# Every SBUF tile that the matmuls read at 32 modulo 256 bytes, in a one-core encoder block

## The chip, the core and the metric

The kernel runs on one core of a Trainium2 chip. The metric is device time in microseconds (us) of one execution; a kernel is run several times and the median is taken. Beside these runs there is one profiled execution, whose trace gives the start and end of each instruction.

## The reference, cut to what matters

One layer over 512 tokens of 1024 features:

```python
x = x + 0.5 * swiglu_ffn(rms_norm(x, ffn1_norm), ffn1_w13, ffn1_w2)      # D_FF = 2816
h = rms_norm(x, mix_norm)
a, g, q, k, v, fl = split(h @ w_in)        # 512 | 512 | 512 | 512 | 512 | 8
y_conv = silu(layer_norm(depthwise_conv31(a * sigmoid(g)) + conv_b))
y_attn = softmax(q k^T / 8 + cum[t] - cum[s], causal) @ v      # 8 heads of 64
#   cum = cumsum(log_sigmoid(fl + forget_b))
y = concat(rms_norm(y_conv, out_norm_conv), rms_norm(y_attn, out_norm_attn))
x = x + y @ w_out
x = x + 0.5 * swiglu_ffn(rms_norm(x, ffn2_norm), ffn2_w13, ffn2_w2)
out = rms_norm(x, final_norm)
```

## The kernel before, in words

**Data.** Features lie on the 128 partitions, tokens along the row. A 512-token row of fp32 is 2048 bytes of a partition. The stream x is eight such tiles. Every matmul operand is kept as two fp32r tiles, a rounded high part and the rest (`xh`/`xl` for the input, `whi`/`wlo` for weights), and a product is the sum of three matmuls for each block of 128 rows: high by high, low by high, high by low. In `product` the weight block (128x128, 512 bytes of a partition) is the operand that is loaded into TensorE (weight load, PEld), and the input row is the one that streams (512 columns, or 256 in `seven`). In `values` it is the other way round: blocks of `xh`/`xl` are loaded and 260 columns of weights stream.

**Weights.** A "unit" is one 512 KB block of weights. SP's queue brings it into one of three `raw` buffers, ScalarE (ACT) casts it into one of two `whi` buffers, VectorE (DVE) subtracts to one of two `wlo` buffers; units take the buffers in turn. The units of `values` hold four blocks of 260 columns, so their rows are 4160 bytes long where all others have 4096.

**Stages**, by the trace's time: both FFNs (about 17 to 365 us and 590 to 950 us) alternate gate and up products (`f1g`, `f1u`, `f2g`, `f2u`: 24 matmuls of 512 columns each) with `seven`, which forms the down projection of eight hidden tiles from seven half-size products (`f1p`, `f2p`: 84 matmuls of 256 columns); the last six hidden tiles go down in plain products (`f1o`, `f2o`). Between them stands the mixer: four `conv_tile`s (`pg`, `pa`), `values` (`pv`), four `attention`s of two heads (`pq`, `pk`, scores `s`, transposes `pt`, output `po`), `conv_norm`, and the output projection (`wo`). Two of the convolutions run on DVE (`conv`), two as ACT taps that POOL adds up (`tap`, `acc`), beside all of `values` and attention.

**Order.** Every operation is recorded first; `Plan.schedule` then emits all engines' streams by priced costs and buffer availability, and each engine runs its stream in order. Matmul products follow each other in the recorded order (`in_turn`).

**Addresses.** The allocator lays tiles out one behind another in the order of their first use: a tag's buffers lie side by side, each as long as the tag's longest tile. The three `raw` buffers start at 36640, which is 32 modulo 256. After them the 4160-byte buffers and the conv inputs `u0` to `u3` (542 columns, 2176 bytes with padding) shift all that follows. In the built program this gives, modulo 256:

| tile | before | changed |
|---|---|---|
| `whi`, two buffers | 224, 32 | 32, 32 |
| `wlo`, two buffers | 96, 160 | 32, 32 |
| `xh0` to `xh7`, `xl1` to `xl7` | 224 | 32 |
| `xl0` | 96 | 32 |
| `vt` (a unit held whole: `w2` in `f1g1`, A22 of `seven`) | 224, both halves | 32, both halves |
| hidden tiles and sums of `seven`, `yh`/`yl`, `q`, `k` | 224, some 96 | 32 |

All blocks inside a tile lie at multiples of 512 bytes from its start, except in `values`, where blocks of 260 columns are 1040 bytes apart. The constants `ones` and `sel` lie at 128 and stay there.

The functions that the change touches, and what calls them:

Of the kernel before, what the change touches and what calls it, by code (L numbers as in the profile page):

```python
# [36 lines left out]
P = 128  # L37
T = 512
D = 1024
KD = D // P  # L40
# [6 lines left out]
DC = 512  # L47
NC = DC // P
TAPS = 31
H = 8  # L50
HD = 64
NT = T // P
VC = 260
# [26 lines left out]
G_CW = 52  # L80
G_FB = G_CW + NC * TAPS
N_G = G_FB + H

# [275 lines left out]
def block_kernel(ctx: ExitStack, tc, x_d, w13a, w2a, wag, wvf, wqk, wo, w13b, w2b, par_d, out_d):  # L359
# [9 lines left out]
    def tile_(shape, tag, name, bufs=1, dt=F32):  # L369
        return plan.tile(sb, shape, dt, tag, name, bufs)  # L370
# [4 lines left out]
    def product_bank(name):  # L375
        return bank("mm", name, 3)
# [40 lines left out]
    def down(w2, js, d):  # L417
        pieces = []
        for j in js:
            half, k = divmod(j, HALF)  # L420
            if pieces and pieces[-1][1] == KD * half + d and pieces[-1][3] == k:
                pieces[-1][3] = k + 1
            else:
                pieces.append([w2, KD * half + d, k, k + 1])
        return pieces

    units = []
    for w13, w2 in ((w13a, w2a), (w13b, w2b)):
        for g in range(len(GROUPS) + 1):
            for i, j in enumerate(GROUPS[g] if g < len(GROUPS) else [None] * (KD // 2)):  # L430
                if j is not None:
                    units += [([(w13, 2 * j + n, 0, KD)], P) for n in range(2)]
                if g and i < KD // 2:
                    units += [(down(w2, GROUPS[g - 1], d), P) for d in (2 * i, 2 * i + 1)]
        if w13 is w13a:
            for piece in ORDER.split():
                n = int(piece[1:] or 0)
                units += {"c": [([(wag, 2 * n + i, 0, KD)], P) for i in range(2)],
                          "v": [([(wvf, i, 0, KD // 2)], VC) for i in range(4)],
                          "a": [([(wqk, 2 * n + i, 0, KD)], P) for i in range(2)],  # L440
                          "n": [], "w": [([(wo, 2 * n + i, 0, KD)], P) for i in range(2)]}[piece[0]]
    taken = [0]
# [115 lines left out]
    def product(ps, w, ah, al):  # L558

        hi, lo = w  # L560
        n = len(ah)
        first = None
        for k in range(n):
            step = plan.join("PE", first)
            if first is None:
                first = step
                if taken[0] > 3 or ready == []:
                    in_turn(step)
            PE.matmul(ps, hi[:, k], ah[k], start=k == 0, stop=False)
            PE.matmul(ps, hi[:, k], al[k], start=False, stop=False)  # L570
            PE.matmul(ps, lo[:, k], ah[k], start=False, stop=k == n - 1)
            plan.join(None)
        stream[:] = [step]
# [208 lines left out]
    def conv_tile(i):  # L782
        pg, pa = product_bank(f"pg{i}"), product_bank(f"pa{i}")
        product(pg, unit(), xh, xl)
        if not mix:
            mix["rstd"] = st.rstd()
        rstd = mix["rstd"]
        gn, an = tile_([P, T], "ew", f"gn{i}", BUFS["ew"]), tile_([P, T], "ew", f"an{i}", BUFS["ew"])
        V.tensor_mul(gn, pg, rstd)
        S.activation(gn, gn, AF.Sigmoid)  # L790
        product(pa, unit(), xh, xl)
        V.tensor_mul(an, pa, rstd)
        u = tile_([P, TAPS - 1 + T], f"u{i}", f"u{i}")
        G.memset(u[:, :TAPS - 1], 0.0)
        V.tensor_mul(u[:, TAPS - 1:], an, gn)
        acc = slot(16 + i, f"acc{i}")
        a = bank("cv", f"conv{i}") if i in DVE_CONV else acc
        for j in range(TAPS):
            w = par[:, G_CW + i * TAPS + j:G_CW + i * TAPS + j + 1]
            bias = par[:, G_CB + i:G_CB + i + 1]  # L800
            if i in DVE_CONV and j == 0:
                V.tensor_scalar(a, u[:, 0:T], w, bias, ALU.mult, ALU.add)
            elif i in DVE_CONV:
                V.scalar_tensor_tensor(a, u[:, j:j + T], w, a, ALU.mult, ALU.add)
            elif j == 0:
                S.activation(a, u[:, 0:T], AF.Identity, scale=w, bias=bias)
            else:
                t = tile_([P, T], "tap", f"tap{i}_{j}", 2)
                S.activation(t, u[:, j:j + T], AF.Copy, scale=w)
                G.tensor_add(a, a, t)  # L810
        if a is not acc:
            S.copy(acc, a)
        plan.urgency = 0.0
        conv[i] = acc


    vt = tile_([P, NT, H * HD], "vt", "vt")
    zf = tile_([P, NT, H], "zf", "zf")
    cum = []

    def values():
        plan.urgency = URGENT_V
        pr = bank("misc", "pr", MISC)
        PE.transpose(pr[:, :P], st.compact, ident)
        rcol = tile_([P, NT], "rcol", "rcol")
        V.tensor_copy(rcol, pr[:, 0:P:32])
        plan.urgency = 0.0
        for c in range(2):
            pv = [product_bank(f"pv{c}_{t}") if t < 2 else bank("s", f"pv{c}_{t}", 2) for t in range(NT)]
            for kh in range(2):  # L830
                hi, lo = unit()
                for t in range(NT):
                    ts_ = slice(t * P, (t + 1) * P)
                    o = pv[t][:, :VC]
                    head = None
                    for k in range(KD // 2):
                        kk = kh * (KD // 2) + k
                        step = plan.join("PE", head)
                        if head is None:
                            head = step  # L840
                            in_turn(step)
                        PE.matmul(o, xh[kk][:, ts_], hi[:, k], start=kk == 0, stop=False)
                        PE.matmul(o, xh[kk][:, ts_], lo[:, k], start=False, stop=False)
                        PE.matmul(o, xl[kk][:, ts_], hi[:, k], start=False, stop=kk == KD - 1)
                        plan.join(None)
                    stream[:] = [step]
            plan.urgency = URGENT_V
            for t in range(NT):
                rc = rcol[:, t:t + 1]
                S.activation(vt[:, t, 4 * HD * c:4 * HD * (c + 1)], pv[t][:, :4 * HD], AF.Copy, scale=rc)  # L850
                V.scalar_tensor_tensor(zf[:, t, 4 * c:4 * c + 4], pv[t][:, 4 * HD:VC], rc,
                                       par[:, G_FB + 4 * c:G_FB + 4 * c + 4], ALU.mult, ALU.add)
            plan.urgency = 0.0

        plan.urgency = URGENT_LF
        lf, e1, e2, e3 = (tile_([P, NT, H], n, n) for n in ("lf", "e1", "e2", "e3"))
        ps = plan.tile(pp, [P, 16, NT, H], F32, "pt", "e", PT)
        p1, p2, p3, p4 = (ps[:, n] for n in range(4))  # L860
        V.scalar_tensor_tensor(e1, zf, -1.0, zf, ALU.mult, ALU.min)
        S.activation(p1, e1, AF.Exp)
        plan.join("V")
        V.tensor_scalar(p2, p1, 2.0, None, ALU.add)
        V.reciprocal(e2, p2)
        V.tensor_mul(p3, p1, e2)
        V.tensor_mul(e1, p1, e2)
        V.tensor_mul(p4, p3, e1)
        V.tensor_scalar(e3, p4, 1.0 / 17.0, None, ALU.mult)
        for n in (15, 13, 11, 9, 7, 5, 3):  # L870
            V.scalar_tensor_tensor(e3, e3, 1.0 / n, p4, ALU.add, ALU.mult)
        V.scalar_tensor_tensor(e3, e3, 1.0, p3, ALU.add, ALU.mult)
        V.tensor_scalar(p2, zf, 0.0, None, ALU.min)
        V.scalar_tensor_tensor(lf, e3, -2.0, p2, ALU.mult, ALU.add)
        plan.join(None)


        for g in range(2):
            lfs = tile_([P, NT, P], "ew", f"lfs{g}", BUFS["ew"])
            G.memset(lfs, 0.0)  # L880
            V.tensor_copy(lfs[:, :, 0::32], lf[:, :, 4 * g:4 * g + 4])
            pc = bank("misc", f"pc{g}", MISC)
            plan.join("PE")
            for t in range(NT):
                PE.transpose(pc[:, t * P:(t + 1) * P], lfs[:, t], ident)
            plan.join(None)
            cs = slot((21, 14)[g], f"cum{g}")
            V.tensor_tensor_scan(cs, one, pc, 0.0, ALU.mult, ALU.add)

            rows = plan.tile(dr, [4, T], F32, f"cum{g}", f"cumd{g}")  # L890
            with plan.urgent(500.0):
                Q.dma_start(out=rows, in_=cs[0::32, :])
            cum.append(rows)

        plan.urgency = 0.0
# [211 lines left out]
```

## Time and profile before

| | |
|---|---|
| median of 3 runs | 967.07 us (966.13 to 968.39) |
| profiled execution | 966.01 us |
| its span in the trace | 964.3 us (1.7 us lie around it) |
| TensorE busy | 945.4 us, 98% of the span |
| DVE, ACT, POOL busy | 664.4, 420.7, 152.5 us |
| DMA | 91.19 MB, mean 95 GB/s |

Matmuls overlap in their pipeline, so a matmul's duration in the trace is longer than the time that it takes of TensorE. What it takes is the distance from its start to the start of the next one. In this text that distance is called a step.

### The profile page before, as it was taken

To read this page: it belongs to the slowest core of one execution; us is meant where nothing else is said; L and a number is where in the kernel's file an instruction comes from. 1 tells how busy PE (TensorE), PEld (TensorE's weight loads), DVE (VectorE), ACT (ScalarE), POOL (GpSimd) and SP (SyncE) were. 2 spreads that over 40 slices of the span, in tenths; PEclk is the share of its full clock that TensorE was granted. 3 is DMA by queue.
4 is the path that set the end of the run, shared out by engine and by line. 5 is a ranking of instruction groups with operands and counts; after the bars stand their busy time and mean duration, and the time that the engine had idled before them with its cause. 6 is when DMAs were issued, how large, how long until landed. Compare 5 with 4: busy or idle time off the path is not lost.

```text
span 964.3 us, 13408 instructions
## 1 busy us (share of the span) xinstructions
PE 945.4 (98%) x5233; PEld 790.3 (82%) x5233; DVE 664.4 (69%) x1050; ACT 420.7 (44%) x656; POOL 152.5 (16%) x134
## 2 busy tenths in 40 slices
PE   9999999999999999998999999999999999999995
PEld 7888888888998888896666777888898888999884
DVE  6655887657777465889988866555777756766454
ACT  7433433334333246666769645333443333333232
POOL 1000211001121001997732000000111001111000
PEclk9999999999999999999999999999999999999998
DMA  7223332223322232222211112223332222332122
GB/s 253 79 87 103 116 108 91 88 88 103 127 99 83 66 111 92 88 89 86 90 67 53 57 67 88 88 93 104 114 106 93 83 89 87 132 110 104 50 66 88
DMA packets 31455, 91.19 MB, mean 95 GB/s; under 512 B 3352, under 2 KB 10648, under 8 KB 31392
## 3 DMA queue, kind: packets, MB, share of 16 engines
q1 hardware_dynamic: 31392, 90.33, 27.6%
q8 instruction: 41, 0.67, 0.3%
q14 instruction: 22, 0.18, 0.1%
HBM read 88.21 MB, written 2.11 MB: 94 GB/s over the span
## 4 chain that ended last, share of the span: by engine, by line
PE 89%; DVE 4%; POOL 3%; ACT 2%; issue 1%; DMA 0%; SPq 0%; DVEq 0%; POOLq 0%; ACTq 0%
PE f2g L235 13%; PE f2u L235 13%; PE f1u L235 13%; PE f1g L235 13%; PE f2p L235 8%; PE f1p L235 8%; PE wo L235 5%; PE f1o L235 3%; PE f2o L235 3%; POOL acc L235 3%; PE pk L235 2%; PE pg L235 1%; PE pq L235 1%; PE pa L235 1%; PE po L235 1%
## 5 line engine op out<-in xcount | busy, mean ns | idle before, releaser
L235 ACT CAST whi<-raw 128x1024 fp32r<-128x1024 f32 (+3 forms) x153 | 151.6, 991 | 311.4 <-issue 135.8
L235 DVE TENSOR_TENSOR wlo<-raw,whi 128x1024 fp32r<-128x1024 f32 (+3 forms) x153 | 185.9, 1216 | 21.5 <-ACT whi L235 18.3
L235 POOL TENSOR_TENSOR acc<-acc,tap 128x512 f32<-128x512 f32 x60 | 89.0, 1485 | 86.8 <-ACT tap L235 83.2
L235 PE MATMUL f1u<-xl,whi 128*128 128x512 f32 x176 | 69.4, 394 | 0.4 <-DVE xl L235 0.3
L235 PE MATMUL f2u<-xh,wlo 128*128 128x512 f32 x176 | 69.7, 396 | 0.0
L235 PE MATMUL f1u<-xh,wlo 128*128 128x512 f32 x176 | 69.6, 396 | 0.0
L235 PE MATMUL f2g<-xh,wlo 128*128 128x512 f32 x176 | 69.6, 396 | 0.0
L235 PE MATMUL f2g<-xl,whi 128*128 128x512 f32 x176 | 69.6, 395 | 0.0
L235 PE MATMUL f1u<-xh,whi 128*128 128x512 f32 x176 | 69.4, 394 | 0.0
L235 PE MATMUL f2g<-xh,whi 128*128 128x512 f32 x176 | 69.2, 393 | 0.0
L235 PE MATMUL f2u<-xh,whi 128*128 128x512 f32 x176 | 69.2, 393 | 0.0
L235 PE MATMUL f2u<-xl,whi 128*128 128x512 f32 x176 | 69.1, 393 | 0.0
L235 PE MATMUL f1g<-xl,whi 128*128 128x512 f32 x168 | 66.6, 396 | 0.0
L235 PE MATMUL f1g<-xh,wlo 128*128 128x512 f32 x168 | 66.5, 396 | 0.0
L235 PE MATMUL f1g<-xh,whi 128*128 128x512 f32 x168 | 66.3, 394 | 0.0
L235 DVE TENSOR_TENSOR f2un<-f2u,rstd_f2in 128x512 f32<-128x512 f32 x22 | 15.2, 691 | 65.8 <-PE f2u L235 65.8
L235 POOL TENSOR_TENSOR f2S<-raw 128x512 f32<-128x512 f32 x8 | 10.4, 1298 | 311.9 <-DMA raw<-w2b 296.9
L235 DVE TENSOR_TENSOR f1un<-f1u,rstd_in 128x512 f32<-128x512 f32 x22 | 15.2, 690 | 55.6 <-PE f1u L235 55.6
L235 ACT ACTIVATE tap<-u,par 128x512 f32<-128x512 f32 x60 | 42.5, 720 | 22.2 <-POOL acc L235 22.1
L235 POOL TENSOR_TENSOR f1S<-raw 128x512 f32<-128x512 f32 x8 | 10.4, 1299 | 263.3 <-DMA raw<-w2a 227.0
L235 DVE SCALAR_TENSOR_TENSOR conv<-u,par,conv 128x512 f32<-128x512 f32 x60 | 44.9, 749 | 0.8
L235 PEld LDWEIGHTS f1u<-xl,whi 128*128 128x128 f32 x176 | 33.0, 188 | 8.9 <-DVE xl L235 1.2
(406 smaller groups left out, 2408.0 us busy)
## 6 DMA issues: line engine op xcount, KB each, us to landing
raw<-w13b SPq DMA_DIRECT2D x44, 512.0 KB, 3.4
raw<-w13a SPq DMA_DIRECT2D x42, 512.0 KB, 3.5
raw<-w2a SPq DMA_DIRECT2D x16, 512.0 KB, 3.5
raw<-w2b SPq DMA_DIRECT2D x16, 512.0 KB, 3.4
raw<-wag SPq DMA_DIRECT2D x8, 512.0 KB, 3.5
raw<-wqk SPq DMA_DIRECT2D x8, 512.0 KB, 3.4
raw<-wo SPq DMA_DIRECT2D x8, 512.0 KB, 3.5
raw<-w2a SPq DMA_DIRECT2D x16, 192.0 KB, 2.4
```

Of the source, the lines that this page charges most:

```text
L235: ins = getattr(target, method)(*real, **kw)
```

## The change

The loads of `values` are cut into eight units of two blocks (`[128, 2, 260]`, 2080 bytes of a partition) in place of four units of four, so that the longest tile in `raw`, `whi` and `wlo` is 4096 bytes; and the conv inputs are allocated with 576 columns (2304 bytes), of which 542 are used as before. Every tile from `raw` on then starts at 32 modulo 256. The arithmetic and the number of matmuls stay as they were; `values` has four more loads, casts and subtractions of half the size.

```diff
+U = 576
...
-                          "v": [([(wvf, i, 0, KD // 2)], VC) for i in range(4)],
+                          "v": [([(wvf, i, k, k + 2)], VC) for i in range(4) for k in (0, 2)],
...
-        u = tile_([P, TAPS - 1 + T], f"u{i}", f"u{i}")
+        u = tile_([P, U], f"u{i}", f"u{i}")[:, :TAPS - 1 + T]
...
-            for kh in range(2):
+            for kh in range(4):
                 hi, lo = unit()
                 for t in range(NT):
...
-                    for k in range(KD // 2):
-                        kk = kh * (KD // 2) + k
+                    for k in range(2):
+                        kk = kh * 2 + k
```

The planner then orders the mixer anew; up to the first matmul of `values` all five streams are as before, but for names. Two places are shown. On ACT, at the start of `values`, before (`whi` is a unit's cast, `tap` a product of a convolution, `gn` a sigmoid):

```order
L235 CAST whi_3586<-raw_3466 128x1040
L235 ACTIVATE gn_3589<-gn_3589 128x512
L235 ACTIVATE tap_18_3601<-u_2775,par 128x512
L235 ACTIVATE tap_19_3606<-u_2775,par 128x512
L235 ACTIVATE tap_20_3620<-u_2775,par 128x512
L235 ACTIVATE tap_21_3631<-u_2775,par 128x512
L235 CAST whi_3640<-raw_3514 128x1040
L235 ACTIVATE tap_22_3657<-u_2775,par 128x512
L235 ACTIVATE tap_23_3685<-u_2775,par 128x512
L235 ACTIVATE tap_24_3704<-u_2775,par 128x512
L235 CAST whi_3713<-raw_3563 128x1040
```

In the changed kernel the same stretch of ACT's stream, up to the fourth half unit:

```order
L236 CAST whi_3586<-raw_3466 128x520
L236 ACTIVATE tap_18_3591<-u_2775,par 128x512
L236 ACTIVATE gn_3589<-gn_3589 128x512
L236 ACTIVATE tap_19_3606<-u_2775,par 128x512
L236 ACTIVATE tap_20_3617<-u_2775,par 128x512
L236 ACTIVATE tap_21_3630<-u_2775,par 128x512
L236 CAST whi_3637<-raw_3514 128x520
L236 ACTIVATE tap_22_3651<-u_2775,par 128x512
L236 CAST whi_3682<-raw_3563 128x520
L236 ACTIVATE tap_23_3687<-u_2775,par 128x512
L236 ACTIVATE tap_24_3712<-u_2775,par 128x512
L236 CAST whi_3720<-raw_3603 128x520
```

The second cast of `values` stands behind tap 21 in both, but there it brings half a unit, and it is needed after half as many matmuls.

On TensorE, behind `values`, where the transposes `pc` of the forget gates (`lfs`) stand among the matmuls of the first key product `pk`, before:

```order
L235 MATMUL pk_4010<-xh_125,whi_3949 128x512
L235 MATMUL pk_4010<-xl_132,whi_3949 128x512
L235 MATMUL pk_4010<-xh_125,wlo_3963 128x512
L235 MATMUL pc_4026<-ident,lfs_3651 128x128 x4
L235 MATMUL pk_4010<-xh_137,whi_3949 128x512
```

In the changed kernel at the same place of TensorE's stream:

```order
L236 MATMUL pk_4035<-xh_125,whi_3980 128x512
L236 MATMUL pk_4035<-xl_132,whi_3980 128x512
L236 MATMUL pk_4035<-xh_125,wlo_3994 128x512
L236 MATMUL pk_4035<-xh_137,whi_3980 128x512
L236 MATMUL pk_4035<-xl_143,whi_3980 128x512
L236 MATMUL pk_4035<-xh_137,wlo_3994 128x512
L236 MATMUL pc_4058<-ident,lfs_3648 128x128 x4
```

The transposes moved behind three more matmuls of `pk`.

## The prediction

> **What bounds the kernel now.** First the page: busy time of the engines, the granted clock in 40 slices, and the chain of work that ended last.
>
> ```profile
> span 964.3 us, 13408 instructions
> ...
> PE 945.4 (98%) x5233; PEld 790.3 (82%) x5233; DVE 664.4 (69%) x1050; ACT 420.7 (44%) x656; POOL 152.5 (16%) x134
> ...
> PEclk9999999999999999999999999999999999999998
> ...
> PE 89%; DVE 4%; POOL 3%; ACT 2%; issue 1%; DMA 0%; SPq 0%; DVEq 0%; POOLq 0%; ACTq 0%
> ```
>
> TensorE is busy nearly throughout at a full clock and makes up 89% of the chain. Then the same by stage (columns: window, its length, busy time and count of each engine, clock, DMA share, GB/s):
>
> ```profile
> 17.60:365.00 347.40, 347.40 (x1841) 297.43 (x1840) 233.78 (x341) 130.72 (x187) 24.45 (x25) 1.00 0.29 98
> 412.00:450.00 38.00, 33.73 (x232) 30.98 (x231) 34.62 (x63) 25.66 (x39) 34.89 (x26) 0.96 0.24 84
> 450.00:590.00 140.00, 137.58 (x893) 99.09 (x892) 116.73 (x243) 93.76 (x183) 42.34 (x36) 1.00 0.21 72
> 590.00:940.00 350.00, 350.00 (x1858) 299.42 (x1851) 224.96 (x327) 123.62 (x176) 21.40 (x16) 1.00 0.28 94
> ```
>
> In both FFNs TensorE never stops, DVE is busy 67% and 64%, DMA below 30%. So there only the step of a matmul counts, and the feeding engines have room for a faster one. In the mixer TensorE stops for 4.3 us in one window (38.00 less 33.73) and for 2.4 us in the next. The chain, in order of time, gives the length of whole products:
>
> ```profile
> 53.00 5.56 PE f1g L235 x24
> 58.56 5.55 PE f1u L235 x24
> ...
> 108.53 10.01 PE f1p L235 x84
> ...
> 129.65 9.91 PE f1p L235 x84
> ...
> 332.57 33.32 PE f1o L235 x144
> ```
>
> A step of 512 columns is 5.555/24 or 33.32/144, both 231.4 ns; one of 256 columns is 9.96/84, 118.6 ns. The program issues 2364 of the first kind in the FFNs (four times 22 products of 24, 144 in `f1o`, 108 in `f2o`), 576 in the mixer (16 products of 24, 192 in `wo`), and 1344 of the second kind (16 times 84).
>
> **Whether the place of an operand matters.** One product in the trace has all its weights at the residue of its input: `f1g1`, whose unit is held in `vt`, both halves at 224, as are `xh` and `xl`. Beside it an ordinary gate product, weights at 224 and 96; starts of first matmuls and of the matmul after the last (columns: start, duration, instruction):
>
> ```profile
> 18.14 0.39 PE L235 MATMUL f1g<-xh,w 128*128 128x512 f32 x1
> ...
> 21.13 0.39 PE L235 MATMUL f1g<-xl,w 128*128 128x512 f32 x1
> ...
> 23.40 0.39 PE L235 MATMUL f1g<-xh,w 128*128 128x512 f32 x1
> 23.62 0.40 PE L235 MATMUL f1u<-xh,whi 128*128 128x512 f32 x1
> ...
> 75.05 0.40 PE L235 MATMUL f1g<-xh,whi 128*128 128x512 f32 x1
> ...
> 80.61 0.39 PE L235 MATMUL f1u<-xh,whi 128*128 128x512 f32 x1
> ```
>
> The uniform product takes 23.62 less 18.14, 5.48 us or 228.3 ns a step, and its last ten steps (21.13 to 23.40) 227 ns. The mixed one takes 5.56 us. Nothing else differs: same shapes, same input, same clock. The products with weights at 32 and 160 (`f1u` above, 5.55) are no faster than those at 224 and 96, so at 512 columns the residue of the weights alone changes nothing; that all are equal does. At 256 columns it is otherwise. Twelve matmuls each: weights at 224 and 96, all at 224 (A22, from `vt`), weights at 32 and 160:
>
> ```profile
> 109.80 0.28 PE L235 MATMUL f1p<-f10h,whi 128*128 128x256 f32 x1
> ...
> 111.22 0.28 PE L235 MATMUL f1p<-f10h,f1S 128*128 128x256 f32 x1
> ...
> 115.53 0.28 PE L235 MATMUL f1p<-f10h,f1A 128*128 128x256 f32 x1
> ...
> 116.96 0.27 PE L235 MATMUL f1p<-f10h,f1S 128*128 128x256 f32 x1
> ...
> 130.90 0.28 PE L235 MATMUL f1p<-f10h,whi 128*128 128x256 f32 x1
> ...
> 132.26 0.28 PE L235 MATMUL f1p<-f10h,f1S 128*128 128x256 f32 x1
> ```
>
> These are 1.42, 1.43 and 1.36 us: 118.3, 119.2 and 113.3 ns a step. Uniform at 224 gains nothing here; weights at 32 and 160 do, by 5.0 ns.
>
> **The change part by part.** No row has the streaming operand anywhere but at 224 or 96 in `product`, so a uniform 32 is an extrapolation.
>
> *512 columns, FFNs.* Ends: 227 ns (settled) and 228.3 (with the first, slower half of `f1g1`, whose first input row `xl0` lies at 96). I take 227.5, the middle, since `xl0` now lies with the rest, while each new product may have to settle: 2364 x (231.4 - 227.5) = 9.2 us less, all on the path.
>
> *512 columns, mixer.* 576 x 3.9 is 2.2 us; TensorE waits there for others at many places, so I count half, 1.1 us less (ends 0 and 2.2).
>
> *256 columns.* The nearest row is the uniform one, 119.2 against the mean 118.6: 1344 x 0.6 = 0.8 us more. The other end is 113.3: 1344 x 5.3 = 7.1 us less.
>
> *Values.* Four units become eight. A cast or subtraction of 520 columns lies between these rows:
>
> ```profile
> L235 ACT CAST whi<-raw 128x1040 fp32r<-128x1040 f32 x4 | 4.2, 1048 | 0.0
> ...
> L235 DVE TENSOR_TENSOR wlo<-raw,whi 128x1040 fp32r<-128x1040 f32 x4 | 4.9, 1237 | 0.0
> ...
> raw<-w2a SPq DMA_DIRECT2D x16, 192.0 KB, 2.4
> ...
> raw<-wvf SPq DMA_DIRECT2D x4, 520.0 KB, 3.4
> ```
>
> With the half at no less than half of these, and a few tenths of fixed cost each, ACT and DVE get some 0.7 us more each (an estimate), in the window where DVE is busy 34.62 of 38 us. The four more loads land in 2.4 to 3.4 us each, no longer than the 2.9 us that TensorE takes for a half unit, and three `raw` buffers run ahead; SP's queue issues them where it issued the large ones, ahead of the same `wqk` loads. What is not hidden is the buffer: there are two `whi`, and the second half unit can be cast only when `pa` has left its buffer, as the first half starts on TensorE, and when ACT has passed tap 21:
>
> ```profile
> 411.98 0.28 PE L235 MATMUL pv<-whi,xh 128*128 128x260 f32 x1
> ...
> 435.49 0.39 PE L235 MATMUL pq<-xh,whi 128*128 128x512 f32 x1
> ...
> 414.96 1.04 ACT L235 CAST whi<-raw 128x1040 fp32r<-128x1040 f32 x1
> ...
> 416.04 1.24 DVE L235 TENSOR_TENSOR wlo<-raw,whi 128x1040 fp32r<-128x1040 f32 x1
> ```
>
> `values` takes 23.51 us for 192 matmuls, 2.94 us a half unit. The first half is done at 414.9; the second's low part is ready when the DVE row of 416.04, halved, is done: about 416.7. TensorE waits 1.8 us, and perhaps 1 us more at the third, whose subtraction stands behind the long `u` product on DVE. So `pq` starts some 2 to 3 us late. Behind it stands the longest wait of the kernel:
>
> ```profile
> 437.71 0.46 ACT L235 ACTIVATE vt<-pv,rcol 128x256 f32<-128x256 f32 x1
> 438.06 1.04 ACT L235 CAST whi<-raw 128x1024 fp32r<-128x1024 f32 x1
> 439.12 1.28 ACT L235 ACT_TABLE_LOAD   x1
> ...
> 446.70 0.43 DVE L235 COPY lfs<-lf 128x16 f32<-128x16 f32 x2
> ...
> 447.10 1.11 PE L235 MATMUL pc<-ident,lfs 128*128 128x128 f32 x4 [4.02 <-DVE lfs L235]
> ```
>
> TensorE stands 4.02 us for the forget gates, whose chain starts with the last `vt` on ACT, 437.71, itself two us behind the last `pv`. Work that reaches this place 2 to 3 us late finds the wait shorter, not the end later. Three more `pk` matmuls now go ahead of `pc` (0.7 us). Ends: 0.7 us less, and 3 us more if the gates' chain is late by as much; I take 0. If the cover goes, the next in line are the rows behind `pc` (`pk`, then the scores of the first head), at the price just given.
>
> *Order of the mixer behind `pc`.* The planner reorders attention and conv_norm. The window 450 to 590 has 2.4 us of idle TensorE: I take 0 with 2.4 us to either side.
>
> *Conv inputs.* Longer tiles, same instructions: nothing.
>
> The sum is -9.2 - 1.1 + 0.8 = -9.5 us on the profiled execution's 966.01, 956.5. The median of the runs is 1.06 us above that execution, so I forecast 957.5.
>
> **A rule that speaks against it.** The Trainium skill, TensorE: Matmul & The Clock Gate, section Back-to-back issue gap, gives a single stream's gap as N/2.4 + 2.5 ns, with no term for where an operand lies; by it the change would save nothing (the second rival below), and a step of 512 columns would be 215.8 ns. The trace does not agree: the steps above are 228 to 231 ns and differ with the place alone.
>
> **Rivals.**
> *The place 32 is itself better.* The 5.0 ns that weights at 32 and 160 gained at 256 columns may come on top at all widths: 5.0 x (2364 + 1344) = 18.5 us, so about 939. For it: the flat 113.3. Against: at 512 columns these weights gained nothing.
> *Nothing happens.* `f1g1` may be fast for another reason: its two halves lie in one tile 4096 bytes apart, and it runs right behind the start-up. Then only the small terms are left: 966 to 967.5. Against: the slow steps of ordinary products occur also late, with an undisturbed stream.
> *Slower: streaming rows at 32 cost.* The streaming operand was never at 32. If starting there costs each matmul what weights at 224 cost against 32, 5.0 ns with no gain from uniformity, it is 5.0 x 3708 = 18.5 us more, about 985.5; from 0.5 ns on, 1.9 us, it makes the kernel measurably slower. For it: no row excludes it. Against: in `values` the streaming weights pass through all residues in steps of 16 bytes and the mean step there, 122 ns for 260 columns, is no longer than that of `f1p` in proportion.
> *Values and the gate chain* are too small to decide: 3 us more, with the main gain, is 960.5.
>
> **How the numbers follow.** The uniform gain as summed: 0.55 (950 to 961). The better place on top: 0.13 (932 to 948). Nothing: 0.18 (964 to 968). Slower: 0.14 (969 to 985). A range from 938 to 967.5 leaves out the lower half of the second case and the last. This kernel's no-change band is 0.2%, 1.9 us. Faster by more: 0.55 + 0.13 + a quarter of the third, 0.72; within: 0.13; slower: 0.15.
>
> **What would show it.** After: `f1g`, `f1u` products of 5.44 to 5.48 us in the chain, in both weight buffers alike; `f1p` at 9.9 to 10.1; `pq` starting later against the end of `pa`, the wait before `pc` shrunk to about 1 to 2 us. The prediction is wrong if the gate and up products stay at 5.55, or if `f1p` and `f1g` shorten both by 5 ns a step.

## The result

The changed kernel takes 960.93 us (median of 6 runs, 958.22 to 961.76) against 967.21 us for the kernel before on the same chip (6 runs, 966.13 to 968.39): a ratio of 0.9932, interval 0.9917 to 0.9946. The forecast was 957.5 us. The profiled execution of after took 961.41 us. From its page, the span, the busy time of the engines and the chain of work that ended last:

```profile
span 959.7 us, 13428 instructions
...
PE 937.7 (98%) x5233; PEld 791.0 (82%) x5233; DVE 671.6 (70%) x1054; ACT 422.1 (44%) x660; POOL 151.5 (16%) x134
...
PE 85%; DVE 9%; ACT 2%; issue 2%; DMA 1%; SPq 0%; DVEq 0%; ACTq 0%
```

TensorE is busy 7.7 us less (945.4 before) for the same 5233 matmuls, but the span is shorter by 4.6 us only. DVE is busy 7.2 us more, and its share of the chain went from 4% to 9%: the end now depends on DVE at places where it did not. The chain of after in order of time (start, length, what):

```profile
32.17 5.44 PE f1g L236 x24
37.61 5.44 PE f1u L236 x24
...
108.33 10.07 PE f1p L236 x84
118.41 5.47 PE f1g L236 x24
...
129.31 10.07 PE f1p L236 x84
...
330.57 32.64 PE f1o L236 x144
363.21 2.04 PE pg L236 x9
...
589.54 0.68 PE f2g L236 x3
...
944.51 0.85 PE rb_out L236 x8
```

Gate and up products are 5.44 us in both weight buffers, where one gave 5.56 and the other 5.55. A step of 512 columns is 32.64/144 or 5.44/24, both 226.67 ns (231.4 before). The 84 matmuls of `seven` take 10.07 us in either buffer (10.01 and 9.91 before): the 113.3 ns steps of the second buffer are gone and nearly all are 120 ns. The rows of the chain of before that mark the same places:

```profile
30.79 5.56 PE f1g L235 x24
...
365.90 2.09 PE pg L235 x9
...
589.14 0.68 PE f2g L235 x3
...
948.36 0.85 PE rb_out L235 x8
```

And around `values` and the transposes of the gates, the timeline of TensorE in after (in brackets the idle time ahead, and what ended it):

```profile
408.46 0.28 PE L236 MATMUL pv<-whi,xh 128*128 128x260 f32 x1
...
413.89 0.39 PE L236 MATMUL pv<-wlo,xh 128*128 128x260 f32 x1 [1.97 <-DVE wlo L236]
...
435.25 0.39 PE L236 MATMUL pq<-xh,whi 128*128 128x512 f32 x1
...
446.44 0.71 PE L236 MATMUL pc<-ident,lfs 128*128 128x128 f32 x4 [2.86 <-DVE lfs L236]
```

From the starts in these rows, and those of `pv` and `pc` before (411.98 and 447.10), the span divides so, in us:

| stretch | before | after | difference |
|---|---|---|---|
| to the second gate product | 30.79 | 32.17 | +1.4 |
| from there to the end of `f1o` | 335.11 | 331.04 | -4.1 |
| convolutions, to the first `pv` | 46.08 | 45.25 | -0.8 |
| `pv` to `pc` | 35.12 | 37.98 | +2.9 |
| `pc` to the first `f2g` | 142.04 | 143.10 | +1.1 |
| FFN2, to `rb_out` | 359.22 | 354.97 | -4.2 |
| to the end | 15.94 | 15.19 | -0.8 |

The two FFNs gave 8.3 us, where 8.4 was forecast (two errors that nearly cancel, see below). The mixer, where a gain of 1.1 was forecast, lost 3.1. The start-up belongs to the execution more than to the kernel: over the profiles of this study the second gate product begins anywhere from 30.7 to 33.0 us.

### The profile page after: what moved, and what is told of

Its sections match the earlier page's. It is cut to its first block, busy times and chain, and to the rows that moved or that the text cites. A ratio compares the mean times of both kernels' runs of the same rounds, so it can differ in the third digit from the quotient of the medians.

```text
span 959.7 us, 13428 instructions
## 1 busy us (share of the span) xinstructions
PE 937.7 (98%) x5233; PEld 791.0 (82%) x5233; DVE 671.6 (70%) x1054; ACT 422.1 (44%) x660; POOL 151.5 (16%) x134
## 4 chain that ended last, share of the span: by engine, by line
PE 85%; DVE 9%; ACT 2%; issue 2%; DMA 1%; SPq 0%; DVEq 0%; ACTq 0%
PE f2g L236 13%; PE f2u L236 12%; PE f1u L236 12%; PE f1g L236 12%; PE f2p L236 8%; PE f1p L236 8%; PE wo L236 4%; PE f1o L236 3%; PE f2o L236 3%; DVE conv L236 3%; DVE wlo L236 2%; PE pk L236 1%; PE s L236 1%; PE pg L236 1%; PE pa L236 1%
## 5 line engine op out<-in xcount | busy, mean ns | idle before, releaser
L236 DVE TENSOR_TENSOR wlo<-raw,whi 128x1024 fp32r<-128x1024 f32 (+3 forms) x157 | 190.0, 1210 | 19.4 <-ACT whi L236 17.5
L236 PEld LDWEIGHTS f1u<-xh,whi 128*128 128x128 f32 x176 | 33.0, 188 | 8.4 <-ACT xh L236 1.5
```

What stands on the lines that cost most here:

```text
L236: ins = getattr(target, method)(*real, **kw)
```

## Whether the place is the cause, and which place

Every kernel below is compared with the kernel before in the same batch (967.1 to 967.3 us there). First the change in two halves. The places alone, with whole units in `values`; the rows of the three weight tags are made 4352 bytes long (17 times 256), so that they keep the residue (the address modulo 256; `block_tile` allocates `[P, ROW]` and uses the first 4 x 260 columns):

```diff
+ROW = 1088
...
-    "v": [([(wvf, i, k, k + 2)], VC) for i in range(4) for k in (0, 2)],
+    "v": [([(wvf, i, 0, KD // 2)], VC) for i in range(4)],
...
-        hi = tile_(shape, "whi", f"whi{n}", SPLITS, F32R)
+        hi = block_tile(shape, "whi", f"whi{n}", SPLITS, F32R)
```

> All operands at 32 modulo 256 as in the changed kernel, but values keeps its four units of four blocks (its raw, whi and wlo tiles are lengthened to 4352 bytes, 17 times 256, of which 4160 are used). Theory A (the equal residue gives the gain of the FFNs, and the halved units of values cost the mixer some 3 to 5 us): gate and up products stay at 5.44 us, the 2.2 us wait at the second unit of values is gone, 956 to 958 us. Rival B (the mixer's loss comes from its rows being reordered at all, not from the halved units): 960 to 962 us, the waits only at other places.

It took 958.47 us (4 runs, 958.43 to 959.06), ratio 0.9911 (0.9897 to 0.9924), 2.5 us less than the changed kernel. Its chain, and the waits of TensorE in the mixer (from 365 to 592 us; us in total, times, longest):

```profile
107.42 10.07 PE f1p L242 x84
117.50 5.47 PE f1g L242 x24
...
329.66 32.64 PE f1o L242 x144
```

```profile
PE pc L242 <- DVE lfs L242: 4.0, 1, 4.0
...
PE pv L242 <- DVE wlo L242: 0.6, 2, 0.4
```

The FFN products are those of after to the hundredth, and the wait of `values` is nearly gone. The time is half a microsecond above what theory A gave and 1.5 us below the range of rival B. The halves alone, at the old addresses (`ROW` of 1040 gives tiles of 4160 bytes as before):

```diff
-U = 576
+ROW = 1040
+U = 542
```

> Addresses as before the change (tiles of raw, whi and wlo 4160 bytes long, conv inputs of 542 columns), but values in eight units of two blocks. Theory A: the FFN products stay at 5.55 us and the mixer loses the 3 to 5 us of waits, without the gain of its own matmuls: 970 to 973 us. Rival B (the halved units cost nothing; the loss in the mixer comes from faster matmuls that wait for others): 966 to 968 us.

969.01 us (11 runs, 967.02 to 970.74), ratio 1.0020 (1.0010 to 1.0029). The chain has the old products, the waits of TensorE in the mixer are new:

```profile
31.53 5.56 PE f1g L242 x24
...
109.28 10.01 PE f1p L242 x84
130.40 9.91 PE f1p L242 x84
```

```profile
PE pc L242 <- DVE lfs L242: 2.8, 1, 2.8
PE pt L242 <- DVE sm L242: 2.7, 1, 2.7
PE pv L242 <- DVE wlo L242: 1.9, 2, 1.7
```

So the two parts of the change work against each other: the places bring 8.7 us, and halving the units of `values` costs 1.8 us by itself and 2.5 us on top of the places. That cost is smaller than was expected (969.01 lies between the ranges of the two theories), but the new waits and the sign are those of theory A.

Next, whether 32 is special. Two kernels are the changed one with a constant tile, `mean`, made 224 and 64 bytes longer, which puts the blocks and rows of all products at 0 and at 96 (the second has 32 + 16 where the diff has 32 + 56):

```diff
-    mean = tile_([P, 32], "mean", "mean")
+    mean = tile_([P, 32 + 56], "mean", "mean")[:, :32]
```

> The changed kernel with everything from raw on 224 bytes further, so that all operands lie at 0 modulo 256. Theory A (only equality counts): steps of 226.7 ns at 512 columns and 120.0 at 256 as in the changed kernel, 959 to 963 us. Rival C (the place itself counts, and a row that starts on a boundary has no first part that is short): 220 ns at 512 and 113.3 at 256, the same 6.7 ns less at both, which is 25 us in the FFNs: 933 to 940 us.

> The changed kernel with everything from raw on 64 bytes further: all operands at 96 modulo 256, which is where before had 96 and 224 modulo 128. Theory A (only equality counts): 226.7 and 120.0 ns, 959 to 963 us. Rival C (the place counts, 32 modulo 128 is better than 96 as it was for the weights at 256 columns before): 5 to 7 ns more a step at one width or both, 967 to 985 us.

At 0: 960.70 us (960.35 to 961.17), ratio 0.9933 (0.9919 to 0.9946). At 96: 961.74 us (959.51 to 962.71), ratio 0.9936 (0.9921 to 0.9951). One row of each chain:

```profile
107.23 10.07 PE f1p L236 x84
```

```profile
108.13 10.07 PE f1p L236 x84
```

Both are the changed kernel again, in time and in products. Of the three common residues tried, none is better than another; that the residue is common is what counts.

## Which operands must share it

The remaining kernels start from the one with whole units (958.47 us). A pad ahead of a tag moves it and all that follows. In all but the first the loaded blocks are laid out ahead of the streaming rows, so that few pads are needed. `PADS` gives the bytes ahead of a tag (the one shown puts all streaming rows at 224), and the tags of `FIRST` get their buffers in that order when `xh0` is allocated:

```diff
+FIRST = [("whi", 1088, 2), ("wlo", 1088, 2), ("vt", 2048, 1)]
+FIRST += [(f"q{a}{b}", 512, 1) for a in "01" for b in "01"] + [(f"u{i}", 576, 1) for i in range(4)]
+PADS = {"xh0": 192}
...
+            if tag == "xh0":
+                while FIRST:
...
```

> The kernel with whole values units (958.47 us, all operands of a product at 32 modulo 256, steps of 226.67 ns at 512 columns and 120.0 ns at 256), with one thing changed: the two `wlo` buffers lie at 160 modulo 256; every streaming row and the other weights stay at 32. Theory A (all operands of a product must share the residue; one third of the steps has another loaded residue): gate and up products go back from 5.44 us to 5.55 us, 231 ns a step, since before it was so with 32 and 160 against a streaming row at 224: 2364 x 4.4 ns is 10.4 us, and the mixer up to 2.5 us; the 384 steps of 256 columns that read `wlo` and `whi` go to 113.3 ns as before (32, 160 there too), 2.6 us less: about 966 to 969. Theory B (only the place of the streaming row counts, and 32 is good where 224 is not): 226.67 ns stay, 958.5.

`PADS = {"wlo": 128, "xh1": 128}`. 968.13 us (10 runs), ratio 1.0008 (0.9999 to 1.0018): the gain is gone with one third of the loaded blocks moved, and theory B falls. Its gate products:

```profile
30.88 5.55 PE f1g L249 x24
```

The 113.3 ns of the old second buffer did not come with its weights' places alone: against streaming rows at 32 `f1p`, whose first 24 matmuls read them, took 10.05 us, 119.6 ns a step.

> The kernel with whole values units, with all loaded blocks (`whi`, `wlo`, `vt`, the seven sums) at 32 modulo 256 and all streaming rows (`xh`, `xl`, hidden rows) at 224; the tiles' order in memory differs for that, the loaded ones first. Theory A1 (the streaming row must share the residue of the loaded block): steps of 512 columns go to about 231 ns, 5.55 us a product: 2364 x 4.4 ns plus up to 2.5 us in the mixer, 969 to 971.5. Theory A2 (it is the loaded blocks that must be equal from one step to the next, the streaming row may lie anywhere): 226.67 ns stay, 958.5. At 256 columns A2 gives 120.0 ns, A1 118 to 119.5 as the rows of before that have equal loaded blocks against another streaming place (118.2) or nearly so, up to 2.4 us less.

971.20 us (970.38 to 971.57), ratio 1.0043 (1.0028 to 1.0058), with all loaded blocks equal. So theory A2 falls too: at 512 columns the streaming row has to share the residue of the loaded block. The chain:

```profile
31.74 5.60 PE f1g L258 x24
...
110.14 9.89 PE f1p L258 x84
...
334.83 33.60 PE f1o L258 x144
```

A step is 233.3 ns at 512 columns, more than before, and 117.7 ns at 256, less than the uniform 120. The two widths want different things.

> The kernel with whole values units; high halves of all loaded blocks at 32 modulo 256, low halves at 160 (`wlo` and the low halves of the seven sums), streaming rows at 224: what the second weight buffer had before, now for every product. If place alone sets the step, the rows of before come back everywhere: 5.55 us for gate and up products (231 ns, 2364 x 4.4 ns, 10.4 us more than 958.47, and up to 2.5 us in the mixer), and 113.3 ns at 256 columns (1152 of 1344 steps, the rest are in `vt` with both halves at 32: 1152 x 6.7 ns is 7.7 us less): 961 to 964. Rival: the 113.3 ns of before hang on the buffer itself or on something else than the place modulo 256: then 120 ns stay at 256 columns, and 969 to 971.5.

`PADS = {"wlo": 128, "xh0": 64}`, with `wlo` and the low sums laid last. 961.78 us (961.35 to 963.87), ratio 0.9951 (0.9936 to 0.9966): the steps of the old second buffer came back with its places, though the tiles lie elsewhere. 512 columns are slow again and 256 fast:

```profile
30.73 5.57 PE f1g L258 x24
...
108.63 9.57 PE f1p L258 x84
```

That is 232 ns and 113.9 ns a step. Since `seven` streams hidden tiles and the gate products stream `xh` and `xl`, each can have what suits it:

> The kernel with whole values units, weights in `whi`, `wlo`, `vt` and the rows `xh`, `xl` at 32 modulo 256 as before in it; the hidden rows at 224, the high halves of the seven sums at 32, the low ones at 160. So products of 512 columns in gate and up stay uniform, and the 768 steps of 256 columns that read sums have what gave 113.3 ns before. If place alone sets the step: 768 x 6.7 ns is 5.1 us less, the other 576 steps of 256 columns 120 to 118 ns (up to 1.2 us less), the 252 steps of `f1o` and `f2o` and the 192 of `wo` stay at 226.67 (theory A2) or go to 231 ns (theory A1: 1.1 us more, up to 2 with `wo`): 952 to 955.5. Rival (113.3 hangs on something else): 958.5 to 960.

`PADS = {"u0": 128, "xh0": 128, "r0": 192}`. 953.97 us (4 runs, 953.15 to 955.76), ratio 0.9868 (0.9851 to 0.9886): 13.3 us less than the kernel before, 4.5 us of them beyond the kernel with whole units. Its chain:

```profile
32.95 5.44 PE f1g L258 x24
...
109.11 9.66 PE f1p L258 x84
...
327.93 33.60 PE f1o L258 x144
```

`f1o` pays 0.96 us for its hidden rows at 224, `f1p` gains 0.41 us sixteen times. Two more runs asked whether the distance counts:

> The kernel with whole values units, all loaded blocks at 32 modulo 256, but the streaming rows `xh`, `xl` at 160 (128 bytes off) and the hidden rows at 96 (64 off). With the rows 192 off (224 against 32) the same layout gave 971.2 us: 231 to 233 ns at 512 columns, 118 at 256. If only equal or unequal counts: gate and up products 231 to 233 ns, `f1o`, `f2o` and `wo` as well, 118 ns at 256 columns: 970 to 972. If the distance counts: other steps, each width and distance with its own; at 128 bytes the better half of the range, 958 to 966, or below 226.67 ns, which would be faster than any layout so far: below 953.

`PADS = {"xh0": 128, "r0": 192}`. 968.40 us (10 runs), ratio 1.0010 (1.0001 to 1.0020): outside both expected ranges, and no faster place. Gate products took 5.57 to 5.58 us (232.1 to 232.5 ns, 128 bytes off), `f1o` 32.97 us (229.0 ns, 64 off), `f1p` 9.89 us:

```profile
334.01 32.97 PE f1o L258 x144
```

64 bytes off is thus better at 512 columns than 128 or 192 (33.60 us for `f1o` at both), so unequal places are not all alike.

> The layout that gave 953.97 us (weights at 32 modulo 256, low halves of the seven sums at 160), with the rows `xh`, `xl` at 64 (32 bytes off the weights, instead of equal) and the hidden rows at 160 (128 off, instead of 192). If only equal or unequal counts at 512 columns: 231 to 233 ns in gate and up products, 2112 x 4.4 to 6 ns more, and the 256 columns as in that layout (114 to 116 ns): 964 to 968. If the distance counts, 32 bytes is the least bad: 227 to 229 ns, and the 256 columns at other values: 954 to 960.

`PADS = {"u0": 128, "xh0": 160, "r0": 96}`. 972.41 us (971.16 to 972.65), ratio 1.0053 (1.0036 to 1.0070), slower than expected by 4 us and the slowest of all: 5.60 us for gate products 32 bytes off, so near is not good, and 9.96 us for `f1p`, whose low sums still lie 128 from the high ones. With low sums 128 bytes from the high ones, streaming rows at 224 gave the fast 256-column step and rows at 160 did not. In one table (step in ns, length of a product in the chain over its matmuls; loaded places are those of the weights, in `f1p` A22 is 32 / 32 throughout, and in the second row its sums are as well):

| loaded, high / low | streaming | 512 columns | 256 columns (mean of `f1p`) |
|---|---|---|---|
| 32 / 32 (also 0, 96) | the same | 226.7 | 119.9 |
| 32 / 160 | 32 | 231.2 | 119.6 |
| 32 / 32 | 64 | 233.3 | not run |
| 32 / 32 | 96 | 229.0 | 117.7 |
| 32 / 32 | 160 | 232.1 to 233.3 | 118.6 (low sums at 160) |
| 32 / 32 | 224 | 233.3 | 117.7 |
| 32 / 160 | 224 | 231.9 | 113.9 |

The high blocks lie at 32 in every row with unequal places, so whether the distance counts or the streaming row's own place was not separated.

The last kernel came from a detail in the timeline of the 953.97 us kernel. `seven` forms its products of twelve matmuls in the order A11, A12, S2, S3, S1, A22, S4: the first two read the weights, those named S the sums, A22 the tile in `vt`. These are the first matmuls of A12, S2, A22 and S4:

```profile
110.36 0.28 PE L258 MATMUL f1p<-f10h,whi 128*128 128x256 f32 x1
...
111.77 0.28 PE L258 MATMUL f1p<-f10h,f1S 128*128 128x256 f32 x1
...
115.88 0.28 PE L258 MATMUL f1p<-f10h,f1A 128*128 128x256 f32 x1
...
117.24 0.28 PE L258 MATMUL f1p<-f10h,f1S 128*128 128x256 f32 x1
```

A12 takes 1.41 us and A22 1.36 us, though both have 32 / 32 against 224.

> The layout that gave 953.97 us, but of the low halves of the seven sums only that of S2 lies at 160 modulo 256, those of S3, S1 and S4 at 32 like the high halves. There the twelve matmuls of A11 and of A12, both halves at 32 against hidden rows at 224, took 117.5 ns a step, and so did all 84 with that place in another layout; S2 went over to 113.3 within its first six steps, and A22, both halves at 32 as well, came behind it and kept 113.3. Theory K (the rhythm is kept from one product to the next until something breaks it): S2 starts it, S3, S1, A22 and S4 keep it, f1p stays at 9.66 us and the time at 954. Theory N (each product has the step of its own places, and A22 is fast for another reason): S3, S1 and S4 go to 117.7 ns, 36 x 4.4 ns is 0.16 us a product, f1p 9.82 us, 16 of them 2.5 us: 956.5.

`FIRST` ends with `u1, u2, u3, u0`; `PADS` as in the 953.97 us kernel. 953.60 us (4 runs, 953.06 to 954.57), ratio 0.9856 (0.9839 to 0.9872), the same time. Its chain has `f1p` as it was:

```profile
107.83 9.66 PE f1p L258 x84
```

Theory K holds: one product of twelve with alternating places sets the rhythm, and four others behind it, all at 32 / 32, keep it. A step is therefore not set by its own operands' places alone, but also by the rhythm it finds. Not every place keeps it: in the kernel before, A12 took 1.36 us in the `f1p` of 9.91 us (the prediction's row at 130.90), but A22 behind the sums, all at 224, took 1.43 us again (from 136.55 to 137.98 us), 119.2 ns a step. What it is in the hardware that makes the places count was not measured.

## Why the mixer lost

What happens in `pv` to `pc` is read off the chain through that window alone, 405 to 446 us, of before, after, and the kernel with whole units. Its shares by line:

```profile
by line: POOL acc L235 52.2%; issue 8.0%; DVE e L235 7.5%; DVE conv L235 7.0%; DVE wlo L235 6.2%; DVE u L235 4.2%; ACT tap L235 3.3%; ACT L235 3.1%; POOL lfs L235 2.6%; ACT whi L235 2.3%; ACT gn L235 1.5%; DVE gn L235 1.5%; POOL k L235 1.3%
```

```profile
by line: DVE conv L236 39.1%; DVE wlo L236 26.8%; issue 15.1%; DVE e L236 7.7%; DVE zf L236 2.6%; DVE lfs L236 2.3%; ACT vt L236 2.1%; DVE gn L236 1.7%; DVE u L236 1.5%; ACT acc L236 1.5%; DVE lf L236 0.5%; DVEq L236 0.2%; DVE an L236 0.2%
```

```profile
by line: POOL acc L242 52.1%; issue 9.3%; DVE e L242 7.5%; PE pk L242 4.2%; DVE conv L242 3.6%; ACT tap L242 3.3%; ACT L242 3.1%; DVE wlo L242 2.9%; PE pc L242 2.7%; POOL lfs L242 2.6%; ACT whi L242 2.3%; ACT gn L242 1.5%; DVE gn L242 1.5%;
```

Before, and with whole units, the chain there leads through POOL's sums; with half units through DVE's `conv` and `wlo`. The group of half subtractions and casts in after, to set beside the 4.9 us of four whole subtractions and the 4.2 us of four whole casts:

```profile
L236 DVE TENSOR_TENSOR wlo<-raw,whi 128x520 fp32r<-128x520 f32 x8 | 8.6, 1080 | 0.0
L236 ACT CAST whi<-raw 128x520 fp32r<-128x520 f32 x8 | 5.0, 619 | 0.0
```

Casts cost 0.8 us more, as estimated. Subtractions cost 3.7 us more where 0.7 was: one of half the columns takes 1080 ns against 1237. In after the last `vt`, from which the gates' chain starts, stands at

```profile
437.29 0.48 ACT L236 ACTIVATE vt<-pv,rcol 128x256 f32<-128x256 f32 x1 [1.41 <-DVE zf L236]
```

28.83 us behind the first `pv`, 25.73 before. The second new wait is at the transposes of the first heads. From the waits of TensorE in the mixer of after (the wait at `pc` is in the timeline above):

```profile
PE pt L236 <- DVE sm L236: 2.6, 1, 2.6
PE pv L236 <- DVE wlo L236: 2.1, 2, 2.0
```

DVE's timeline at that place, after and before:

```profile
464.23 3.59 DVE L236 TENSOR_SCALAR sm<-sm,st 128x256 f32<-128x256 f32 x3
```

```profile
464.71 1.94 DVE L235 TENSOR_SCALAR sm<-sm,st 128x256 f32<-128x256 f32 x2
```

The planner, given other units, put three scalings in a row where two stood, and the second `pt` waits for them. The kernel with half units at the old addresses has the same wait (2.7 us), the one with whole units has none: it comes from the halving, not from the places.

A stop can cost more than its length, for the granted clock of TensorE was lower behind some of them. The 4 us behind `pc` before, and the 4 us behind that second `pt` in after (window, length, busy time and count of each engine, clock, DMA share, GB/s):

```profile
447.10:451.10 4.00, 4.00 (x14) 3.38 (x15) 4.00 (x5) 1.39 (x2) 3.84 (x3) 0.63 0.12 39
467.96:471.96 4.00, 4.00 (x9) 2.13 (x10) 3.50 (x11) 2.08 (x6) 0.76 (x1) 0.65 0.01 2
```

By these clocks 1.5 and 1.4 us of work at full clock were lost there (an estimate, 4 us times what is missing to 1.00), and 1.7 us behind `pc` in after (0.57). The second loss is new; it lies in the stretch from `pc` to `f2g`, which lost 1.1 us in all. It is not part of every such stop: with half units at the old addresses the clock stayed at 1.00 behind the same wait. Differences of a microsecond between single profiled executions of the mixer should be read with this in mind.

## Why the prediction was right or wrong

The mechanism and the way the time moved were right, and 6.3 us of the 9.6 forecast from median to median came; most of the difference lies in the mixer.

- *512 columns, FFNs:* right, a little too small. 226.67 ns from the second product on in place of 227.5; products do not settle anew, save 0.03 us behind each `seven` (5.47). By the step it is 2364 x 4.73 = 11.2 us, where 9.2 was forecast.
- *256 columns:* the sign and the nearer row were right, the size too small: 10.07 less 9.96, sixteen times, is 1.8 us lost for 0.8. The two errors nearly cancel, so it is luck that the sum for the FFNs came out to a tenth (8.4 us forecast, 8.3 measured).
- *512 columns, mixer:* 1.1 us forecast, 0.8 came in the convolutions, nothing behind them. With whole units `pv` to `pc` and `pc` to `f2g` took 35.77 and 142.40 us, no less than before: other engines end those stretches.
- *Values:* the wait at the second half unit was forecast with place and size (1.8 us, measured 1.97), the third's smaller (0.16 for about 1), and `pq` starts 3.3 us later against the first `pv` (26.79 and 23.51), 2 to 3 forecast. The step that failed is the next one: "Work that reaches this place 2 to 3 us late finds the wait shorter, not the end later". The wait did shrink, from 4.02 to 2.86 us, but the end came later all the same, since the gates' chain hangs on the last product of `values` and was late by as much (3.1 us at `vt`). That end, 3 us more, had been named and not taken. Under it lies the DVE price: halves of a subtraction were taken at half its duration and a few tenths.
- *Order behind `pc`:* 0 taken, 1.1 us measured, inside the 2.4 given. The wait at `pt` was not named, nor a lower clock behind a stop.
- *Rivals:* 32 is not itself better (0 and 96 give the same), a streaming row at 32 costs nothing, and something did happen. One argument against the slower rival does not hold as written: 118.6 ns for 256 columns is 120.5 in proportion for 260, so the 122 ns of `values` were a little longer, not "no longer"; the measurement decided it. *Values and the gate chain*, 960.5, is the rival that came true beside the main gain.
- *The rule that speaks against it:* the Trainium skill, TensorE: Matmul & The Clock Gate, Back-to-back issue gap, has no place for the operands' addresses in its gap of N/2.4 + 2.5 ns. The forecast took that for a stream's gap; the section calls it the gap of an isolated matmul, and for a stream of weight loads and matmuls it gives about 131 ns at 512 columns. The runs agree with neither: the same instruction streams at full clock took 226.7 to 233.3 ns at 512 columns and 113.3 to 120 ns at 256 with nothing but addresses changed, none of them at the 215.8 and 109.2 that the formula gives (an estimate).

## What to carry to other kernels

Where TensorE streams without a stop, list the SBUF address residue of both operands of each product and compare steps by residue; in this kernel, whose products are in fp32r, equal residues were best at 512 columns and one particular unequal arrangement at 256, and choosing the places with padding and the order of the tiles was worth 13.7 us of 967. Get the addresses with padding, not by cutting the work differently: the cut here handed back 2.5 us through another engine. When a stage is late by some microseconds and a wait stands behind it, look at where the awaited chain itself starts before counting the wait as cover.

## What was unexpected

- Steps keep a rhythm. At 256 columns the same places (32 / 32 against 224) ran at 117.5 ns behind a 512-column product and at 113.3 ns behind a product with alternating places.
- The means of whole products lie between two ends at each width: 226.67 and 233.33 ns at 512 columns, 113.3 and 120.0 at 256, each pair some 6.7 ns apart, with 229 to 232.5 and 117.7 to 119.6 between.
- A subtraction of 520 columns on DVE took 0.69 to 1.73 us, four of eight over 1 us, where four of 1040 columns took 1.23 to 1.24. Why was not tried.
